# A transformer-layer kernel: unread squares written to SBUF instead of PSUM, the attention transposes one weight tile later, a selection step one chunk earlier

## The chip, the cores and the metric

The kernel runs on one core of one Trainium2 chip. The metric is the device time of one execution in microseconds (us), given as the median over runs. A core has several engines that run their own instruction streams and meet at semaphores: PE (TensorE: matmuls and transposes), DVE (VectorE), ACT (ScalarE), POOL (GpSimd) and SP (here it only issues transfers between device memory and SBUF, the on-chip memory). Matmuls write to PSUM, which has eight banks.

## The reference

One layer of a flow-matching backbone is computed for 384 tokens: 128 context tokens and 256 latent tokens, in three blocks of 128. The width is 2048.

```python
mod = silu(cond) @ ada_w + ada_b           # six modulation vectors per token group
h   = rmsnorm(x) * (1 + scale) + shift     # "ada": scale and shift out of mod
q, k, v, o, gates, u = split(h @ w_in)     # 8 heads x 128; u feeds the pooling
for each head and each of two directions:  # chunkwise mLSTM, chunks of 128
    s   = (q k^T) * exp(dmat - m_t)
    num = g * (q C) + s v                  # "inter" and "intra" part
    den = g * (q n) + sum(s)
    h_d = num / max(|den|, exp(-m_t))
    C   = g_state * C + wk^T v             # new state
h_head = rmsnorm(h_fwd + h_bwd) * w
mix = concat(h_head * sigmoid(o), pooled(u)) @ w_out
x   = x + gate * rmsnorm(mix)
y   = x + gate2 * rmsnorm(relu(rmsnorm_mod(x) @ w1)**2 @ w2)
```

All is in 32-bit floats. To keep that precision on TensorE, each large operand is split into a rounded high part and a remainder, and each product is made of three matmuls: high with high, high with low, low with high.

## The kernel before, in words

**Splitting and weights.** `load_w` (line 114) loads one weight tile of up to 128x1024 numbers into a `raw` buffer (three of them) through SP. ACT copies it to the rounded `hi` tile (L126), DVE subtracts to get `lo` (L127). PE then runs the three products: L394 to L396 in the first stage, L135 to L137 elsewhere. In `gemm_T` (line 158) one weight tile gives 24 matmuls of 128x384 results, and after each weight tile the function calls its *feeds*: generators that each emit the next piece of some other work, up to their next `yield`. So the attention, the modulation vectors and the pooling are woven between the weight tiles of the large products.

**Who sets the order.** The order of each engine's instructions up to line 379 is written by hand. From there a scheduler orders them for each engine, on the basis of the order in which the code emits them and of its own estimates. Buffers that are used in turn (tiles with `bufs=N`, and the eight PSUM banks that `bank` hands out) add waits: whoever takes a buffer again waits for its last user.

**The stages.**

1. Up to about 40 us: loads, transposes of x, the first modulation step.
2. To about 190 us: eight steps over the contraction index, each with five chunks of weights: u_0, u_512, v_0, v_3, v_6 (list `chunks`, line 345). The operand of step s+1 is made by `make_h` (line 347, called at L400 after chunk v_3): it scales and shifts by `mod`, with high parts `hh` from ACT (L358) and low parts `hl` from DVE (L359). `mod` for that step comes from `ada_mat` (line 203), which is resumed `ADA_STEPS[ci]` times after chunk number ci. With (4, 0, 4, 1, 0) that is four weight pieces with their matmuls (L221) after u_0, four after v_0, and one last step after v_3. The step that loads the eighth piece also ends with the copy of the sums to SBUF, `ada_sb` (L226, ACT). The last, ninth step is two small selection matmuls (L229) and `ada_finish` (DVE, L237).
3. To about 265 us: q and k of head pair 0, with the pooling and the gates.
4. To about 408 us: q and k of pairs 1, 2 and 3, with the attention of pairs 0, 1 and 2 as a feed; to about 498 us: the four `o` products, the attention of pair 3 in the first two of them.
5. To about 634 us: the output projection (`wo`), then the MLP to the end.

Through stages 4 and 5 a second feed, `ada_vec` (line 247), makes further modulation vectors on DVE (L268, 1.1 us each).

**One attention pair** (`attention`, line 544) has two heads, `hl` 0 and 1. After each weight tile of the pair's q and k products (four tiles each), it emits one piece: decays (`mb` matmuls L561, exponentials L563); scores and keys; the same for the third block; state updates and `outputs(0)`; `outputs(1)`; `outputs(2)`; an empty piece; the transposes. Then a last piece is empty, and `fa.finish()` (L704) emits whatever is left before the next pair begins.

`outputs(i)` (line 609) takes for each head a bank `num` and, for i > 0, a bank `inter`. PE writes the intra sums to `num` (L616) and the inter sums to `inter` (L623); ACT scales the latter into an SBUF tile `nsb` (L625), and DVE adds `num` to it (L626). After that `num` of PSUM is read no more. DVE and ACT make the denominator (L628 to L630) and the normalised sum `hs` (L631, L632). L633 then squares `hs` on ACT, for the sum of squares in `ssh`; its elementwise result is never read, and goes to the free end of the bank `num`, columns 260 to 387. The sums become a reciprocal root (DVE L187, POOL L188), and DVE scales `hs` by it (L635). The transposes `hT` (L670, three blocks for each of two heads) turn `hs` for the output projection, and ACT copies them out as `hnT` (L672).

Of the kernel before, what the change touches and what calls it, by code (L numbers as in the profile page):

```python
# [9 lines left out]
AF = mybir.ActivationFunctionType  # L10
# [6 lines left out]
NTOK = 384  # L17
NH = 8
M = 1024
# [8 lines left out]
N_W = 4  # L28
N_ADA = 4
N_E = 1  # L30
ADA_STEPS = (4, 0, 4, 1, 0)
X_ORDER = "tatatatabtatatatat"
N_X = 2
RATES = (1.5, 1.3, 1.3)
# [4 lines left out]
def hymba_kernel(  # L39
# [6 lines left out]
    nc = tc.nc  # L46
    w_in, w_out, w1, w2, ada_w = w_in[0], w_out[0], w1[0], w2[0], ada_w[0]
# [10 lines left out]
    def bank(name):  # L58
        return psum.tile([P, 512], F32, tag="ps", name=name)
# [74 lines left out]
    def mm3(ps, lh, ll, rh, rl, start, stop):  # L134
        nc.tensor.matmul(ps, lh, rh, start=start, stop=False)  # L135
        nc.tensor.matmul(ps, lh, rl, start=False, stop=False)  # L136
        mm3.ins = nc.tensor.matmul(ps, ll, rh, start=False, stop=stop).ins  # L137

    def wview(w):
        return w.rearrange("(k p) n -> p k n", p=P)  # L140
# [17 lines left out]
    def gemm_T(w, cols, xs, n, evac, feeds=(), korder=(0, 1, 2, 3), name="g", hold=None):  # L158

        wv = wview(w)  # L160
        acc = {}
        for g, c0 in enumerate(cols):
            for o in range(2):
                acc[g, o] = bank(f"acc_{name}_{c0}_{o}")
        for ki, kc in enumerate(korder):
            for g, c0 in enumerate(cols):
                hi, lo = load_w([(0, wv[:, 4 * kc:4 * kc + 4, c0:c0 + 256])], f"{name}_{c0}_{kc}", after=hold(ki, g) if hold else ())
                for k in range(4):
                    xh, xl = xs(4 * kc + k)
                    for o in range(2):  # L170
                        mm3(acc[g, o][:, 0:n], hi[:, k, o * P:(o + 1) * P], lo[:, k, o * P:(o + 1) * P],
                            xh[:, 0:n], xl[:, 0:n], ki == 0 and k == 0, ki == 3 and k == 3)
                for f in feeds:
                    f()
        for g, c0 in enumerate(cols):
            for o in range(2):
                evac(c0 // P + o, acc[g, o])
# [7 lines left out]
    def rstd_cols(out, ss, n, scale):  # L185

        nc.vector.tensor_scalar(out, ss, scale, EPS, op0=ALU.mult, op1=ALU.add)  # L187
        nc.gpsimd.tensor_tensor(out, out, mhalf[:, 0:n], op=ALU.pow)  # L188
# [193 lines left out]
    for s in range(NS):  # L382
        for ci, (kind, c0, w) in enumerate(chunks):
# [6 lines left out]
            for k in range(nk):  # L390
                xh, xl = h[k0 + k]
                for i in range(3):
# [3 lines left out]
                    nc.tensor.matmul(acc[i][:, 0:n], xl[:, sl], hi[:, k, :], start=False, stop=k == nk - 1)  # L396
            for _ in range(ADA_STEPS[ci]):
                next(ada0, None)
# [14 lines left out]
    hx = lambda k: h[k]  # L413
# [117 lines left out]
    ssh = vp.tile([P, 3, 8], F32, name="ssh")  # L531
# [12 lines left out]
    def attention(hp):  # L544
# [64 lines left out]
        def outputs(i):  # L609
            hs = att.tile([P, 2, P], F32, tag="hs", name=f"hs_{hp}_{i}", bufs=3)  # L610
            for hl in range(2):
                hd = h0 + hl
                ps = bank(f"num_{hp}_{i}_{hl}")
                num = ps[:, 0:260].rearrange("p (d e) -> p d e", e=130)[:, :, 0:129]
                for d in range(2):
                    nc.tensor.matmul(num[:, d], e[:, d, hl, i, :], vsb[i][:, hd, :], start=True, stop=True)  # L616
                if i > 0:
                    pi = bank(f"inter_{hp}_{i}_{hl}")
                    iv = pi[:, 0:260].rearrange("p (d e) -> p d e", e=130)[:, :, 0:129]
                    intra, num = num, att.tile([P, 2, 129], F32, tag="num", name=f"nsb_{hp}_{i}_{hl}", bufs=2)  # L620
                    for d in range(2):
                        cs = C0[d] if tokc[d][1] == i else C1[d]
                        nc.tensor.matmul(iv[:, d], q_sb[hd][:, i * P:(i + 1) * P], cs[:, hl, :], start=True, stop=True)  # L623
                    for d in range(2):
                        nc.scalar.activation(num[:, d], iv[:, d], AF.Copy, scale=gcol[:, i, d, hd:hd + 1])  # L625
                    nc.vector.tensor_tensor(num, num, intra, op=ALU.add)  # L626
                dn = att.tile([P, 2], F32, tag="dn", name=f"dn_{hp}_{i}_{hl}", bufs=4)
                nc.scalar.activation(dn, num[:, :, 128], AF.Abs)  # L628
                nc.vector.tensor_tensor(dn, dn, ecol[:, i, hd, :], op=ALU.max)
                nc.vector.reciprocal(dn, dn)  # L630
                nc.scalar.activation(hs[:, hl, :], num[:, 0, 0:128], AF.Copy, scale=dn[:, 0:1])  # L631
                nc.vector.scalar_tensor_tensor(hs[:, hl, :], num[:, 1, 0:128], dn[:, 1:2], hs[:, hl, :], op0=ALU.mult, op1=ALU.add)  # L632
                nc.scalar.activation(ps[:, 260:388], hs[:, hl, :], AF.Square, accum_out=ssh[:, i, hd:hd + 1])  # L633
            rstd_cols(rsh[:, i, h0:h0 + 2], ssh[:, i, h0:h0 + 2], 2, 1.0 / P)
            nc.vector.tensor_tensor(hs, hs, rsh[:, i, h0:h0 + 2].unsqueeze(2).to_broadcast([P, 2, P]), op=ALU.mult)  # L635
            hss[i] = hs
# [17 lines left out]
        for d, wk in enumerate((wk00, wk01)):  # L654
            o = update(0, d, wk)
            nc.gpsimd.dma_start(new_C[0, 0, d, h0:h0 + 2].rearrange("h k e -> k h e"), o[:, :, 0:128])
            nc.vector.tensor_copy(nout[:, d, h0:h0 + 2], o[:, :, 128])
        C1[0] = update(1, 0, wk10)
        C1[1] = update(2, 1, wk21)
        outputs(0)  # L660
        yield
        for i in (1, 2):
            outputs(i)
            yield
        yield
        for hl in range(2):
            hd = h0 + hl
            ps = bank(f"hT_{hp}_{hl}")
# [6 lines left out]
    def mid_vec():  # L675
        for i, q in ((4, 0), (4, 1), (3, 0), (3, 1), (2, 0)):
            yield from ada_vec(i, 1024 * q, 1024, att)

    ada1 = Feed(ada_mat([(2, 8 + 2 * b, 2) for b in range(4)]), RATE_MAT)
    ada2 = Feed(mid_vec(), RATES[0])  # L680

    def qk(g, feeds):
        gemm_T(w_in, [g * 256], hx, NTOK, evac_q, feeds, name="q")
        gemm_T(w_in, [M + g * 256], hx, NTOK, evac_k, feeds, name="k")
# [13 lines left out]
    pre_scope.close()  # L698
    att_scope = ExitStack()
    att = att_scope.enter_context(tc.tile_pool(name="att", bufs=2))  # L700
    for g in range(1, 4):
        fa = Feed(attention(g - 1), 1.0)
        qk(g, (fa, ada1, ada2))
        fa.finish()  # L704


    ada2.rate = RATES[1]
# [8 lines left out]
    def split_pool():  # L716
        for k in range(8, 16):
            mixs[k] = split_T(mix[k][:, 0:NTOK], f"mx{k}")
            mix[k] = None
            yield  # L720

    fa, fs = Feed(attention(3), 1.0), Feed(split_pool(), 1.0)
    for g in range(4):
        gemm_T(w_in, [3 * M + g * 256], hx, NTOK, evac_o, (fa if g < 2 else fs, ada1, ada2), name="o")
        if g == 1:
            fa.finish()
    fs.finish()

    ps = bank("ps_nout")
# [367 lines left out]
```

## Time and profile before

| what | value |
|---|---|
| runs | 1741.73, 1744.26, 1746.68 us; median 1744.26 |
| profiled execution: own time | 1740.87 us |
| profiled execution: span from the first to the last instruction | 1739.2 us |
| busy: PE / DVE / ACT / POOL | 97% / 62% / 36% / 9% of the span |
| mean granted TensorE clock | 0.996 of full speed |

A row of a timeline gives the start on the span's clock, the time that the group took, the engine, the line of the kernel, and the operation with what it writes and reads (`out<-in`); in brackets stands how long the engine was idle before it and what released it. "PEld" is the loading of weights into the array, which overlaps with the matmuls. A row of the waits names who waited, for whom, the total in us, how often, and the longest. A row of the windows gives the busy time and the count of each engine in a stretch of the span, then the mean granted clock (`PEclk`), the mean share of the DMA engines that was busy, and the rate in GB/s.

### The profile page before, as it was taken

What the parts mean: (1) busy time and instruction counts of PE and PEld (TensorE: products, weight loads), DVE (VectorE), ACT (ScalarE), POOL (GpSimd) and SP (SyncE); (2) the same over time, 40 slices, a digit from 0 to 9 for tenths busy, and PEclk for the clock granted to TensorE, in tenths of its full rate; (3) what the DMA queues carried; (4) which work ended last, traced back from release to release, by engine and by line L of the source; (5) the groups of instructions that cost most, each with busy time, mean ns of one, the idle gap of its engine ahead of it and who ended that gap; (6) DMA issues with size and microseconds to landing.
All of it is one profiled execution on the core that took longest, in us unless ns stands there. A gap on an engine that the chain in (4) does not pass through costs nothing.

```text
span 1739.2 us, 24241 instructions
## 1 busy us (share of the span) xinstructions
PE 1695.3 (97%) x9461; PEld 1528.6 (88%) x9461; DVE 1084.5 (62%) x1620; ACT 630.4 (36%) x1050; POOL 150.5 (9%) x186
## 2 busy tenths in 40 slices
PE   6999999999999999999999999999999999999997
PEld 3888898988899989989988988988988988998986
DVE  3677759787889959997347543457444444443446
ACT  4422344545433336443322322322322332332332
POOL 0000002211002223530000000000000000000100
PEclk9999999999999999999999999999999999999999
DMA  9888857776668893755446534444444435434543
GB/s 300 292 291 292 286 164 238 229 227 220 222 216 265 267 317 114 217 162 181 122 125 187 160 122 133 122 148 151 125 122 131 124 122 174 130 121 143 173 133 108
DMA packets 235266, 320.71 MB, mean 184 GB/s; under 512 B 14368, under 2 KB 177808, under 8 KB 234768
## 3 DMA queue, kind: packets, MB, share of 16 engines
q1 hardware_dynamic: 227760, 303.61, 55.6%
q0 software_dynamic: 5728, 13.69, 2.9%
q10 hardware_dynamic: 1664, 1.87, 0.3%
q8 instruction: 74, 1.21, 0.3%
q14 instruction: 40, 0.33, 0.1%
HBM read 308.61 MB, written 10.51 MB: 183 GB/s over the span
## 4 chain that ended last, share of the span: by engine, by line
PE 77%; DVE 9%; DMA 6%; issue 6%; POOL 1%; ACT 1%; SPq 0%; DVEq 0%; POOLq 0%; ACTq 0%
PE y L901 10%; PE y L902 10%; PE y L903 10%; PE acc_w L136 9%; PE acc_w L137 9%; PE acc_w L135 9%; DVE ada_acc L268 4%; PE ada L221 2%; DMA raw_u<-in_w_in_dram 1%; DMA raw_v<-in_w_in_dram 1%; PE acc_q L135 1%; PE acc_o L135 1%; PE acc_q L136 1%; PE acc_q L137 1%; PE acc_o L137 1%
## 5 line engine op out<-in xcount | busy, mean ns | idle before, releaser
L127 DVE TENSOR_TENSOR lo_w<-raw_w,hi_w 128x1024 fp32r<-128x1024 f32 x256 | 313.3, 1224 | 404.2 <-ACT hi_w L126 403.7
L126 ACT ACTIVATE hi_w<-raw_w 128x1024 fp32r<-128x1024 f32 x256 | 271.1, 1059 | 563.9 <-PE y L903 273.1
L136 PE MATMUL acc_w<-h2l,hi_w 128*128 128x384 f32 (+1 forms) x1024 | 346.2, 338 | 0.5 <-DVE h2l L857 0.5
L137 PE MATMUL acc_w<-h2h,lo_w 128*128 128x384 f32 (+1 forms) x1024 | 345.5, 337 | 0.0
L135 PE MATMUL acc_w<-h2h,hi_w 128*128 128x384 f32 (+1 forms) x1024 | 343.7, 337 | 0.7 <-ACT h2h L853 0.6
L268 DVE SCALAR_TENSOR_TENSOR ada_acc<-ada_raw,sg,ada_acc 128x1024 f32<-128x1024 f32 (+1 forms) x240 | 257.2, 1108 | 2.8 <-DMA ada_raw<-in_ada_w_dram 2.7
L135 PEld LDWEIGHTS acc_w<-h2h,hi_w 128*128 128x128 f32 x1024 | 192.2, 188 | 2.3 <-ACT h2h L853 1.5
L136 PEld LDWEIGHTS acc_w<-h2l,hi_w 128*128 128x128 f32 x1024 | 192.5, 188 | 1.7 <-DVE h2l L857 0.8
L137 PEld LDWEIGHTS acc_w<-h2h,lo_w 128*128 128x128 f32 x1024 | 192.4, 188 | 0.1
L806 DVE TENSOR_TENSOR z<-z 128x384 f32<-128x384 f32 x54 | 30.0, 556 | 53.6 <-ACT z L805 53.4
L925 DVE TENSOR_TENSOR y<-y,y 128x512 f32<-128x512 f32 x81 | 55.6, 691 | 11.3 <-PE y L903 10.9
L126 ACT ACTIVATE hi_wo<-raw_wo 128x1024 fp32r<-128x1024 f32 x32 | 34.0, 1063 | 77.3 <-DMA raw_wo<-in_w_out_dram 37.5
L819 POOL DMA_DIRECT2D gf_dram<-gfT x1 | 0.5, 521 | 669.3 <-DVE gfT L818 669.3
L805 ACT ACTIVATE z<-acc_w 128x384 f32<-128x384 f32 x54 | 26.3, 488 | 75.7 <-PE acc_w L137 75.7
L394 PE MATMUL v<-hi_v,hh 128*128 128x384 f32 (+1 forms) x144 | 47.7, 332 | 0.0
L221 PE MATMUL ada<-ada_raw,cT 128*32 128x256 f32 x672 | 46.0, 395 | 1.1 <-DMA ada_raw<-in_ada_w_dram 1.1
L127 DVE TENSOR_TENSOR lo_wo<-raw_wo,hi_wo 128x1024 fp32r<-128x1024 f32 x32 | 41.0, 1292 | 9.2 <-ACT hi_wo L126 8.8
L396 PE MATMUL v<-hi_v,hl 128*128 128x384 f32 (+1 forms) x144 | 46.5, 323 | 0.0
L395 PE MATMUL v<-lo_v,hh 128*128 128x384 f32 (+1 forms) x144 | 46.5, 323 | 0.0
L135 PE MATMUL acc_o<-hh,hi_o 128*128 128x384 f32 x128 | 44.8, 350 | 0.0
L135 PE MATMUL acc_q<-hh,hi_q 128*128 128x384 f32 x128 | 44.7, 349 | 0.0
L135 PE MATMUL acc_k<-hh,hi_k 128*128 128x384 f32 x128 | 44.4, 347 | 0.0
(957 smaller groups left out, 3634.5 us busy)
## 6 DMA issues: line engine op xcount, KB each, us to landing
raw_w<-in_w_dram SPq DMA_DIRECT2D x256, 512.0 KB, 3.8
ada_raw<-in_ada_w_dram SPq DMA_DIRECT2D x188, 512.0 KB, 4.8
raw_wo<-in_w_out_dram SPq DMA_DIRECT2D x32, 512.0 KB, 5.0
raw_u<-in_w_in_dram SPq DMA_DIRECT2D x16, 512.0 KB, 7.9
raw_q<-in_w_in_dram SPq DMA_DIRECT2D x16, 512.0 KB, 4.5
raw_k<-in_w_in_dram SPq DMA_DIRECT2D x16, 512.0 KB, 5.0
raw_o<-in_w_in_dram SPq DMA_DIRECT2D x16, 512.0 KB, 4.7
raw_v<-in_w_in_dram SPq DMA_DIRECT2D x16, 384.0 KB, 8.1
```

What stands on the lines that cost most here:

```text
L126: nc.scalar.activation(hi[:, 0:n], raw[:, 0:n], AF.Copy)
L127: low = lambda: nc.vector.tensor_tensor(lo[:, 0:n], raw[:, 0:n], hi[:, 0:n].bitcast(F32), op=ALU.subtract)
L135: nc.tensor.matmul(ps, lh, rh, start=start, stop=False)
L136: nc.tensor.matmul(ps, lh, rl, start=False, stop=False)
L137: mm3.ins = nc.tensor.matmul(ps, ll, rh, start=False, stop=stop).ins
L221: nc.tensor.matmul(ps[32 * g:32 * g + 32, 0:w], cT[:, j, 6 - 2 * b:38 - 2 * b], raw[:, a, :], start=b == 0 and j < 4, stop=b == n - 1 and ...
L268: nc.vector.scalar_tensor_tensor(acc[:, g, :], raw[:, a, :], cj, acc[:, g, :], op0=ALU.mult, op1=ALU.add)
L394: nc.tensor.matmul(acc[i][:, 0:n], xh[:, sl], hi[:, k, :], start=k == 0, stop=False)
L901: nc.tensor.matmul(acc, xh[:, s], hi, start=k == 8 * ch, stop=False)
L902: nc.tensor.matmul(acc, xh[:, s], lo, start=False, stop=False)
L903: nc.tensor.matmul(acc, xl[:, s], hi, start=False, stop=k == 8 * ch + 7)
L925: nc.vector.tensor_tensor(dst, acc[i], dst, op=ALU.add)
```

## The change

Three things are changed.

- **The scratch of the squares.** For i > 0, L633 writes the unread squares to the SBUF tile `nsb` (the half that L632 has just read), where it wrote them to the PSUM bank `num`. The bank is then free after DVE's addition L626. For i = 0, `num` is the PSUM bank itself, and nothing changes.
- **The transposes.** `attention` has one more `yield` ahead of the transposes, so a pair now takes nine pieces. The pairs' feeds are kept in the list `fa`, the last two are passed on to each pair of products, and `fa.finish()` is gone. The ninth piece comes after the first weight tile of the *next* product, beside the next pair's first piece.
- **The selection.** `ADA_STEPS` is (4, 0, 5, 0, 0): the ninth step of `ada_mat` comes after chunk v_0, right behind the eighth; `make_h` stays after chunk v_3.

The lines behind the inserted `yield` have a number higher by one: `hT` is L671 in the changed kernel, `hnT` L673.

```diff
-ADA_STEPS = (4, 0, 4, 1, 0)
+ADA_STEPS = (4, 0, 5, 0, 0)
...
-                nc.scalar.activation(ps[:, 260:388], hs[:, hl, :], AF.Square, accum_out=ssh[:, i, hd:hd + 1])
+                nc.scalar.activation(num[:, 1, 0:128] if i > 0 else ps[:, 260:388], hs[:, hl, :], AF.Square, accum_out=ssh[:, i, hd:hd + 1])
...
             outputs(i)
             yield
         yield
+        yield
         for hl in range(2):
...
+    fa = []
     for g in range(1, 4):
-        fa = Feed(attention(g - 1), 1.0)
-        qk(g, (fa, ada1, ada2))
-        fa.finish()
+        fa.append(Feed(attention(g - 1), 1.0))
+        qk(g, (*fa[-2:], ada1, ada2))
...
-    fa, fs = Feed(attention(3), 1.0), Feed(split_pool(), 1.0)
+    fa.append(Feed(attention(3), 1.0))
+    fs = Feed(split_pool(), 1.0)
     for g in range(4):
-        gemm_T(w_in, [3 * M + g * 256], hx, NTOK, evac_o, (fa if g < 2 else fs, ada1, ada2), name="o")
-        if g == 1:
-            fa.finish()
+        gemm_T(w_in, [3 * M + g * 256], hx, NTOK, evac_o, (*fa[2:], *((fs,) if g >= 2 else ()), ada1, ada2), name="o")
```

**PE at the end of attention pair 0.** Before: the last matmul of k (`acc_k`), then the transposes `hT` of the blocks 0 and 1, then the first matmuls of the next pair's q (`acc_q`), then the transposes of block 2.

```order
L137 MATMUL acc_k_1_2888<-hh_1864,lo_k_3_3080 128x384
L670 MATMUL hT_0_3107<-cst,hs_0_2845 128x128
L670 MATMUL hT_0_3107<-cst,hs_1_2919 128x128
L670 MATMUL hT_1_3113<-cst,hs_0_2845 128x128
L670 MATMUL hT_1_3113<-cst,hs_1_2919 128x128
L135 MATMUL acc_q_0_3131<-hh_262,hi_q_0_3135 128x384
L136 MATMUL acc_q_0_3131<-hl_263,hi_q_0_3135 128x384
L137 MATMUL acc_q_0_3131<-hh_262,lo_q_0_3136 128x384
L135 MATMUL acc_q_1_3132<-hh_262,hi_q_0_3135 128x384
L136 MATMUL acc_q_1_3132<-hl_263,hi_q_0_3135 128x384
L670 MATMUL hT_0_3107<-cst,hs_2_2991 128x128
L670 MATMUL hT_1_3113<-cst,hs_2_2991 128x128
```

In the changed kernel the 24 matmuls of q's first weight tile come first; these are the last of them and what follows (`mb` are the next pair's decays).

```order
L137 MATMUL acc_q_1_3120<-hh_496,lo_q_0_3124 128x384
L671 MATMUL hT_0_3151<-cst,hs_0_2845 128x128
L671 MATMUL hT_0_3151<-cst,hs_1_2919 128x128
L671 MATMUL hT_0_3151<-cst,hs_2_2991 128x128
L671 MATMUL hT_1_3157<-cst,hs_0_2845 128x128
L671 MATMUL hT_1_3157<-cst,hs_1_2919 128x128
L671 MATMUL hT_1_3157<-cst,hs_2_2991 128x128
L561 MATMUL mb_0_0_3171<-mrow,pick 128x384
L561 MATMUL mb_0_1_3176<-mrow,pick 128x384
L561 MATMUL mb_1_0_3181<-mrow,pick 128x384
L135 MATMUL acc_q_0_3119<-hh_719,hi_q_1_3203 128x384
L136 MATMUL acc_q_0_3119<-hl_720,hi_q_1_3203 128x384
```

The first transposes moved back by 24 matmuls and the last two by 19. The other three pairs move alike; for pairs 2 and 3 the product that follows is one of the `o` products.

**PE in the u and v stage, step 2.** Before: the end of the 18 matmuls of chunk v_3 (the tile `v_2_2` of them), then the selection L229, then chunk v_6.

```order
L394 MATMUL v_2_2_922<-hi_v_2_916,hh_724 128x384
L395 MATMUL v_2_2_922<-lo_v_2_917,hh_724 128x384
L396 MATMUL v_2_2_922<-hi_v_2_916,hl_725 128x384
L229 MATMUL ada_6_800<-cst,ada_sb_6_909 128x4 x2
L394 MATMUL v_2_0_974<-hi_v_2_970,hh_719 128x288
```

In the changed kernel: the end of the modulation matmuls L221, the first three matmuls of chunk v_3, and then the selection.

```order
L221 MATMUL ada_6_800<-ada_raw_6_12_903,cT 32x256 x4
L394 MATMUL v_2_0_925<-hi_v_2_921,hh_719 128x384
L395 MATMUL v_2_0_925<-lo_v_2_922,hh_719 128x384
L396 MATMUL v_2_0_925<-hi_v_2_921,hl_720 128x384
L229 MATMUL ada_6_800<-cst,ada_sb_6_909 128x4 x2
L394 MATMUL v_2_1_926<-hi_v_2_921,hh_719 128x384
```

The selection moved ahead by 15 of the 18 matmuls. It reads `ada_sb`.

**ACT at the same place.** Before: the copy of the last chunk's weights, `ada_sb`, the copy of the next step's first u weights (`hi_u_3`), the four parts of `hh`, the second u weights.

```order
L126 ACTIVATE hi_v_2_970<-raw_v_2_967 128x576
L226 ACTIVATE ada_sb_6_909<-ada_6_800 128x256
L126 ACTIVATE hi_u_3_1003<-raw_u_3_1001 128x1024
L358 ACTIVATE hh_947<-hm_946,mod 128x128
```

In the changed kernel:

```order
L126 ACTIVATE hi_v_2_970<-raw_v_2_967 128x576
L126 ACTIVATE hi_u_3_1003<-raw_u_3_1001 128x1024
L226 ACTIVATE ada_sb_6_909<-ada_6_800 128x256
L126 ACTIVATE hi_u_3_1058<-raw_u_3_1056 128x1024
L358 ACTIVATE hh_947<-hm_946,mod 128x128
```

`ada_sb` now stands behind the copy of the next step's first u weights, in each of steps 2 to 6. On SP the loads moved with it: before, one u tile and two v tiles follow the first half of the modulation pieces, one v tile and one u tile the second half; in the changed kernel the three v tiles follow the first half and the two u tiles the second.

## The prediction

> **What bounds the kernel now.** I read the page's head first, then PE's waits, then a table of windows, then the timeline around each wait.
>
> ```profile
> span 1739.2 us, 24241 instructions
> PE 1695.3 (97%) x9461; PEld 1528.6 (88%) x9461; DVE 1084.5 (62%) x1620; ACT 630.4 (36%) x1050; POOL 150.5 (9%) x186
> ```
>
> PE works for all but 43.9 us of the span. No matmul of weights is taken away here, so the change can gain only what PE idles, or what it runs below full clock. The waits of PE between 40 and 600 us say how much lies near the change:
>
> ```profile
> PE hT L670 <- DVE hs L635: 7.1, 4, 2.3
> PE inter L623 <- ACT num L633: 5.3, 4, 2.3
> PE u L394 <- ACT hh L358: 1.9, 1, 1.9
> PE acc_wo L137 <- DVE lo_wo L127: 0.9, 2, 0.8
> ```
>
> The columns are total, count and longest. The transposes wait once for each of the four attention pairs (7.1 us in all); `inter`, whose bank L633 still writes, four times (5.3); the first u matmul once, for `hh` (1.9). Together that is 14.3 us. The windows show which stages are tight for DVE, and where the clock falls:
>
> ```profile
> 40.00:160.00 120.00, 119.91 (x871) 97.19 (x870) 82.26 (x169) 39.93 (x66) 1.26 (x3) 1.00 0.90 294
> 280.00:320.00 40.00, 36.41 (x239) 33.92 (x238) 36.31 (x65) 20.33 (x61) 11.45 (x9) 1.00 0.77 241
> 320.00:360.00 40.00, 37.72 (x246) 35.29 (x245) 29.96 (x63) 18.16 (x50) 7.01 (x7) 0.97 0.68 211
> 360.00:400.00 40.00, 38.75 (x252) 37.45 (x252) 34.88 (x55) 18.45 (x55) 7.94 (x8) 0.99 0.76 235
> 400.00:440.00 40.00, 38.10 (x241) 35.58 (x239) 29.24 (x52) 18.41 (x45) 5.23 (x5) 0.96 0.65 207
> 440.00:480.00 40.00, 36.57 (x230) 34.16 (x229) 36.75 (x58) 18.70 (x47) 3.06 (x3) 1.00 0.71 230
> 520.00:560.00 40.00, 39.10 (x224) 38.21 (x226) 40.00 (x32) 14.65 (x22) 10.29 (x5) 1.00 0.84 267
> ```
>
> After the window's length come PE, PEld, DVE, ACT and POOL, then clock, DMA share and GB/s. In pairs 1 and 2 (320 to 440 us) DVE has 5 to 11 us to spare in 40. In pair 0 (280 to 320) and pair 3 (440 to 480) it has about 3.5, and at 520 to 560, in the output projection, none.
>
> **Part 1: the transposes, one weight tile later.** Pair 1 in the timeline:
>
> ```profile
> 354.78 0.60 PE L670 MATMUL hT<-cst,hs 128*128 128x128 f32 x4
> 355.49 1.66 POOL L188 TENSOR_TENSOR rsh<-rsh,mhalf 128x2 f32<-128x2 f32 x1 [8.13 <-DVE rsh L187]
> 357.18 0.42 DVE L635 TENSOR_TENSOR hs<-hs,rsh 128x256 f32<-128x256 f32 x1 [0.58 <-POOL rsh L188]
> 357.66 0.69 PE L670 MATMUL hT<-cst,hs 128*128 128x128 f32 x2 [2.28 <-DVE hs L635]
> 358.47 0.52 PE L136 MATMUL acc_q<-hl,hi_q 128*128 128x384 f32 x1
> 358.79 0.52 PE L137 MATMUL acc_q<-hh,lo_q 128*128 128x384 f32 x1
> 361.18 0.34 PE L136 MATMUL acc_q<-hl,hi_q 128*128 128x384 f32 x1
> 361.36 0.34 PE L137 MATMUL acc_q<-hh,lo_q 128*128 128x384 f32 x1
> ```
>
> PE reaches the transposes at 354.78, and the last scaled `hs` is there at 357.60 (357.18 + 0.42). At full clock the matmuls start 0.18 us apart (361.18, 361.36). The 24 that now stand ahead take about 24 x 0.175 = 4.2 us, against 2.3 us of stall, so in pair 1 the wait is gone. Right after the stall matmuls start 0.32 us apart (358.47, 358.79): the clock is about half. Its price follows from the windows: 320 to 360 lacks 0.03 of 40 us and 360 to 400 lacks 0.01, so 1.6 us; 400 to 440, with the stall of pair 2, lacks 0.04, again 1.6 us. Without the stalls I expect neither dip. The weight load of the transpose loses some 0.2 us more. Pair 1: 2.3 + 0.2 + 1.6, about +4.1.
>
> A rule of the Trainium skill bears on the dips ("TensorE: Matmul & The Clock Gate", section "Why this matters for your kernels"): the clock halves after about 3 us without matmuls. By that rule stalls of 2.3 us would not cost the clock, and the sum would be 3.2 us smaller if the dips had another cause and stayed; the row of 358.47 stands directly behind the stall, and I go by it.
>
> Pairs 0, 2 and 3, by the rows of PE that waited and what they waited for:
>
> ```profile
> 292.29 0.75 DVE L626 TENSOR_TENSOR nsb<-nsb,num 128x258 f32<-128x258 f32 x2
> 293.76 0.39 PE L616 MATMUL num<-v,e 128*128 128x129 f32 x2
> 295.97 0.28 ACT L633 ACTIVATE num<-hs 128x128 f32<-128x128 f32 x1 [0.17 <-DVE hs L632]
> 296.43 0.71 PE L623 MATMUL inter<-C,q 128*128 128x129 f32 x4 [2.28 <-ACT num L633]
> 306.13 0.60 PE L670 MATMUL hT<-cst,hs 128*128 128x128 f32 x4
> 307.96 0.42 DVE L635 TENSOR_TENSOR hs<-hs,rsh 128x256 f32<-128x256 f32 x1 [0.59 <-POOL rsh L188]
> 308.44 0.44 PE L670 MATMUL hT<-cst,hs 128*128 128x128 f32 x2 [0.83 <-DVE hs L635]
> 389.41 0.71 PE L623 MATMUL inter<-C,q 128*128 128x129 f32 x4 [1.25 <-ACT num L633]
> 407.36 0.66 PE L670 MATMUL hT<-cst,hs 128*128 128x128 f32 x4 [1.90 <-DVE hs L635]
> 442.29 0.71 PE L623 MATMUL inter<-C,q 128*128 128x129 f32 x4 [1.30 <-ACT num L633]
> 461.06 0.44 PE L670 MATMUL hT<-cst,hs 128*128 128x128 f32 x2 [2.13 <-DVE hs L635]
> ```
>
> **Part 2: the scratch of the squares.** In pair 0 PE waits from 294.15 to 296.43 for L633 (295.97), while DVE's last read of that bank, L626, ended at 293.04 (292.29 + 0.75). With the scratch in SBUF this wait ends before PE arrives, so 2.3 us go; in pairs 2 and 3 likewise 1.25 and 1.30. The fourth wait, the rest of the 5.3 us (0.5), is at a block with i = 0, which is unchanged. L633 took 0.28 us into PSUM; into SBUF I bound it by L631's 0.40, the next rows' ACT tile of that size: 0.1 us x 16 on an engine that is half idle (20.33 of 40 us), so nothing on the path, or 1.9 us if all were.
>
> ```profile
> L633 ACT ACTIVATE num<-hs 128x128 f32<-128x128 f32 x24 | 6.7, 279 | 14.3 <-DVE hs L632 14.3
> L631 ACT ACTIVATE hs<-nsb,dn 128x128 f32<-128x128 f32 x16 | 6.3, 396 | 3.1 <-DVE dn L630 3.0
> ```
>
> By pair, then. **Pair 0:** 2.3 + 0.2 (weight load) for `inter`. PE then comes 2.5 us earlier and meets the transposes at 306.13 - 2.5 + 4.2 = 307.8, but DVE, busy without a pause here, still has `hs` at 308.4 or a little before. I leave 0.3 us of stall of the 0.83 + 0.2: 2.5 + 0.7 = +3.2. **Pair 2:** 1.25 + 0.2, 1.90 + 0.2 and the clock 1.6: +5.1. **Pair 3:** 1.30 + 0.2, 2.13 + 0.2: 3.8 at its own place, but DVE follows without slack into the output projection, where PE already waits for `lo_wo` (0.9 us). PE that arrives earlier will wait there for the same DVE instruction; I keep 0.5 (bounds 0 and 3.8).
>
> A new wait of part 1: the bank of the fourth `mb` of the next pair is the one that ACT reads for `hnT`, just behind the transposes. The scheduler set that `mb` two matmuls later (0.35 us); the two `hnT` copies take 1.05 us together at 358.17. I take 0.15 us x 3 = -0.5 (bounds 0 and -1.6).
>
> **Part 3: the selection, 15 matmuls earlier.** The gain is the `hh` wait of 1.9 us in the last step, plus about 0.3 of lighter waits for `lo_u`: `mod` is there earlier and `make_h` runs ahead. The price lies on ACT and SP: `ada_sb` now stands behind the copy `hi_u` of the next step, which waits for its load. A step of before:
>
> ```profile
> 112.09 1.93 PE L221 MATMUL ada<-ada_raw,cT 128*32 128x256 f32 x32
> 113.46 0.68 ACT L126 ACTIVATE hi_v<-raw_v 128x576 fp32r<-128x576 f32 x1 [8.04 <-DMA raw_v<-in_w_in_dram]
> 114.09 0.39 ACT L226 ACTIVATE ada_sb<-ada 128x256 f32<-128x256 f32 x1
> 114.68 1.06 ACT L126 ACTIVATE hi_u<-raw_u 128x1024 fp32r<-128x1024 f32 x1 [0.20 <-DMA raw_u<-in_w_in_dram]
> ```
>
> PE ends the modulation matmuls at 114.02 and three matmuls later, at 114.6, wants the selection. If `raw_u` lands as before (114.68), `hi_u` ends at 115.74, `ada_sb` at 116.13, and PE stalls some 1.6 us. But the load of v_6 (295 KB) no longer stands ahead of it, which at the window's 294 GB/s is 1.0 us, and the swap in the first half (a 295 KB tile for one of 524 KB) brings the modulation pieces up to 0.8 us forward. The stall is then 0 to 0.6 us, I take 0.3, and five steps are so ordered: -1.5. Part 3 in all: 2.2 - 1.5 = +0.7 (bounds -5.8, with 1.6 us in each of the five, and +2.2).
>
> **The sum.** 3.2 + 4.1 + 5.1 + 0.5 - 0.5 + 0.7 = 13.1 us. The profiled execution's own time, 1740.87 us, becomes 1727.8. The median of the runs is 1744.26, 3.4 us above that execution, and on it the forecast is 1731.2.
>
> **Rivals.** *All of it counts.* DVE catches up in the o stage, pair 3 keeps its 3.8, and the selection never waits: 3.3 + 1.5 + 0.5 more, a gain of 18.4, 1725.9. For it: DVE idles in 400 to 440 (29.24 of 40). Against: 40.00 of 40 at 520 to 560.
>
> *DVE is the bound behind the transposes.* The transposes wait again one weight tile later since DVE, with PE earlier, is late by what was won before. Kept would be the `inter` waits of pairs 0 and 2 (2.5 + 1.5) and one tile's cover in pair 1 (2.5), less part of the rest: 6.5 us, 1737.8. For it: 36.31 busy of 40 in pair 0. Against: 29.96 and 29.24 in pairs 1 and 2.
>
> *Slower: the selection stalls PE in the u and v stage.* There PE has no idle now (119.91 of 120), and the loads run at 0.90 of the DMA engines. If raw_u lands as late as before, five stalls of 1.6 us come; if each brings a clock dip of 1.6 us as the stall of 357.66 did, and delays the release of the `ada` buffers and with it the next loads by as much again, the price is 5 x (1.6 + 1.6 + 1.6) = 24 us, against 14.6 us of gains elsewhere (13.1 + 1.5): slower by 9, 1753. It decides from a loss of 3 us a step on. Against: raw_u gets a shorter queue ahead of it.
>
> *The change doesn't do what it says.* If the bank of `num` were held by another reader, the `inter` waits would stay: 13.1 - 2.5 - 1.5 = 9.1 us, 1735.2. The order of instructions leaves L626 as the last user, so little speaks for it.
>
> **How the numbers follow.** A measurement tells some 0.3%, 5.2 us, from no change. I give 0.55 to the forecast with its bounds (gain 9 to 16), 0.16 to the full gain, 0.17 to DVE as the bound (a third of it within 5.2 us), 0.05 to the bank that stays held, 0.07 to stalling selections (0.04 slower, 0.03 about even). Faster: 0.55 + 0.16 + 0.11 + 0.05 = 0.87; same: 0.06 + 0.03 = 0.09; slower 0.04. The range goes from the full gain with some margin, 1724, to DVE as the bound, 1738.
>
> **What would show it.** Right: `inter` waits for L633 only at i = 0 (0.5 us); `hT` waits for `hs` under 1 us in all; PEclk 1.00 in all windows from 320 to 440; the waits for `lo_wo` up by 2 to 3 us; selections that wait 0.3 us behind `ada_sb`, and no wait of u for `hh`. Wrong: waits of `hT` above 3 us in all (DVE), PE under 116 of 120 us in the window 40 to 160 (selection), or a clock under 1.00 where no stall stands.

## The result and the profile after

The changed kernel takes 1733.32 us (median of 6 runs, 1730.40 to 1734.16) against 1742.99 us before (median of 6, 1738.11 to 1746.68). The ratio is 0.9944, with a 95% interval from 0.9925 to 0.9963: 9.7 us faster. The forecast was 1731.2, a gain of 13.1.

The head of the profile after, whose execution took 1733.51 us:

```profile
span 1731.8 us, 24241 instructions
PE 1693.1 (98%) x9461; PEld 1527.8 (88%) x9461; DVE 1082.6 (63%) x1620; ACT 629.1 (36%) x1050; POOL 150.6 (9%) x186
```

PE's idle time fell from 43.9 to 38.7 us. PE's waits between 25 and 640 us, in total, count and longest (left out are 1.4 us for `lo_u` and 1.0 of `ps_col`, both as before, and 0.4 for a load of a modulation piece):

```profile
PE ada L229 <- ACT ada_sb L226: 4.4, 4, 1.4
PE inter L623 <- ACT num L633: 2.0, 2, 1.2
PE acc_wo L137 <- DVE lo_wo L127: 1.0, 2, 0.8
PE inter L623 <- DVE C L606: 0.9, 1, 0.9
PE acc_k L135 <- ACT C L603: 0.8, 1, 0.8
PE mb L561 <- ACT hnT L673: 0.5, 1, 0.5
```

The 7.1 us of the transposes and the 1.9 of `hh` are gone, and `inter` waits 2.0 us for L633 where it waited 5.3. New are 4.4 us of the selection and 2.2 us behind the states C and `hnT`. The windows of the changed kernel, columns as before:

```profile
40.00:160.00 120.00, 117.92 (x841) 95.22 (x844) 81.05 (x167) 38.04 (x63) 1.25 (x3) 0.99 0.88 288
160.00:200.00 40.00, 37.57 (x248) 31.07 (x241) 28.37 (x62) 12.51 (x20) 0.00 (x0) 0.96 0.80 266
280.00:320.00 40.00, 39.41 (x256) 37.63 (x255) 37.02 (x63) 20.29 (x61) 7.93 (x7) 1.00 0.77 239
320.00:360.00 40.00, 40.00 (x271) 37.27 (x270) 32.12 (x68) 19.80 (x54) 11.69 (x9) 1.00 0.74 236
360.00:400.00 40.00, 37.08 (x244) 35.13 (x244) 36.35 (x56) 18.96 (x57) 7.56 (x8) 1.00 0.78 242
400.00:440.00 40.00, 39.28 (x259) 36.48 (x258) 32.98 (x59) 20.77 (x54) 5.62 (x6) 1.00 0.67 216
440.00:480.00 40.00, 40.00 (x249) 38.19 (x248) 38.50 (x58) 18.72 (x45) 3.06 (x3) 1.00 0.80 254
```

The clock is at 1.00 from 280 to 480 us, and short in the u and v stage instead (0.99 of 120 us, 0.96 of 40). PE has full windows at 320 and 440; it has lost ground at 40 to 160 (117.92 against 119.91) and in pair 2 (37.08 against 38.75).

By stage, from the starts of first matmuls in the timelines: from the first u matmul to the k product of pair 1 (the u and v stage and the products up to the window of pair 0; called the first stretch below) the execution before took 250.3 us and the one after 256.6; from there to the output projection 216.4 and 205.0; from there to the end 1241.2 and 1239.5. So the attention gave 11.4 us, and in these two executions the first stretch took 6.2 back. That last number is too large for the change: with the order of before, the first stretch took from 250.3 to 256.3 us in nine executions (that of before and eight of the experiments), 253.0 in the mean, and the one of before is the shortest. The spread goes with the clock: the executions that met no dip to half clock there took 250.3 to 251.2 us (three), those with one dip 253.0 to 253.7 (four), those with two 255.6 and 256.3. The one after met two. This is why the two profiled spans lie 7.4 apart and the medians 9.7.

### The profile page after: what moved, and what is told of

It is laid out like the page before. It is cut to its first block, busy times and chain, and to the rows that moved or that the text cites. A ratio compares the mean times of both kernels' runs of the same rounds, so it can differ in the third digit from the quotient of the medians.

```text
span 1731.8 us, 24241 instructions
## 1 busy us (share of the span) xinstructions
PE 1693.1 (98%) x9461; PEld 1527.8 (88%) x9461; DVE 1082.6 (63%) x1620; ACT 629.1 (36%) x1050; POOL 150.6 (9%) x186
## 4 chain that ended last, share of the span: by engine, by line
PE 76%; DVE 9%; DMA 8%; issue 4%; ACT 1%; POOL 1%; SPq 0%; DVEq 0%; ACTq 0%; POOLq 0%
PE y L901 10%; PE y L903 10%; PE y L902 10%; PE acc_w L135 9%; PE acc_w L136 9%; PE acc_w L137 9%; DVE ada_acc L268 4%; DMA raw_u<-in_w_in_dram 3%; PE acc_o L135 1%; PE acc_o L137 1%; PE acc_o L136 1%; PE acc_q L135 1%; PE acc_q L137 1%; DMA raw_v<-in_w_in_dram 1%; PE acc_q L136 1%
## 5 line engine op out<-in xcount | busy, mean ns | idle before, releaser
L268 DVE SCALAR_TENSOR_TENSOR ada_acc<-ada_raw,sg,ada_acc 128x1024 f32<-128x1024 f32 (+1 forms) x240 | 258.2, 1111 | 0.8 <-DMA ada_raw<-in_ada_w_dram 0.7
L925 DVE TENSOR_TENSOR y<-y,y 128x512 f32<-128x512 f32 x81 | 55.5, 691 | 11.1 <-PE y L903 10.8
L805 ACT ACTIVATE z<-acc_w 128x384 f32<-128x384 f32 x54 | 26.3, 488 | 75.5 <-PE acc_w L137 75.5
L221 PE MATMUL ada<-ada_raw,cT 128*32 128x256 f32 x672 | 45.7, 392 | 1.6 <-DMA ada_raw<-in_ada_w_dram 1.5
```

Source lines behind the costliest of these rows:

```text
L268: nc.vector.scalar_tensor_tensor(acc[:, g, :], raw[:, a, :], cj, acc[:, g, :], op0=ALU.mult, op1=ALU.add)
L925: nc.vector.tensor_tensor(dst, acc[i], dst, op=ALU.add)
```

## The experiments

Theory 1, formed from the profile after: the attention's gain comes from the transposes; the squares gain little, since what they free is waited for again one step later, at the transposes, by the chain through DVE; the selection loses, since `ada_sb` stands behind a copy that waits for a load. The rival: the terms add, as the prediction summed them. All ratios are to the kernel before, run beside it on the same chip; its medians beside the three groups of experiments were 1742.85, 1742.95 and 1744.67 us.

**One part at a time.** The selection alone:

```diff
-ADA_STEPS = (4, 0, 4, 1, 0)
+ADA_STEPS = (4, 0, 5, 0, 0)
```

> Before, with only the selection moved (ADA_STEPS (4, 0, 5, 0, 0)). Theory 1 (the selection stalls): PE waits 4 to 5 us for ada_sb between 60 and 190 us, one or two stretches of half clock (1.6 us each) follow, the hh wait of 1.9 us is gone: 6 us slower than before, 1.003 to 1.004. Rival (the stalls seen in the changed kernel are given back later, as PE waits less in the attention): within 2 us of before, 0.999 to 1.001.

Measured: 1742.74 us, ratio 1.0002 (0.9988 to 1.0016). The stalls are there, but not the 6 us: by the time the rival was closer. PE's waits of the profiled execution, in which `ada_sb` takes 5.0 us and `hh` none:

```profile
PE hT L670 <- DVE hs L635: 5.9, 3, 2.1
PE ada L229 <- ACT ada_sb L226: 5.0, 5, 2.7
PE inter L623 <- ACT num L633: 4.5, 4, 2.3
```

The profiled execution took 256.0 us for the first stretch, 3.0 more than the mean of the order of before; the waits of the attention were a little shorter. For the u and v stage alone, from the first u matmul to the first q matmul, it took 178.8 us, and the changed kernel 179.4; the nine executions with the order of before took 173.2 to 177.6, 175.3 in the mean.

The squares alone:

```diff
-                nc.scalar.activation(ps[:, 260:388], hs[:, hl, :], AF.Square, ...)
+                nc.scalar.activation(num[:, 1, 0:128] if i > 0 else ps[:, 260:388], hs[:, hl, :], AF.Square, ...)
```

> Before, with only the unread squares moved to SBUF. Theory 1 (DVE sets when the transposes can run): the inter waits go (5.3 to about 1 us), but in pairs 0, 2 and 3 the transposes wait longer by nearly as much (7.1 to 10 or 11 us): 1 us faster, 0.999 to 1.000, and the clock dips stay. Rival (the terms add): 5 us faster, 0.997, transposes still wait 7 us.

Measured: 1743.35 us, ratio 1.0001 (0.9989 to 1.0013). The wait of `inter` in pair 0 went and the transposes waited longer, as theory 1 has it:

```profile
PE hT L670 <- DVE hs L635: 9.6, 4, 3.2
PE inter L623 <- ACT num L633: 1.3, 2, 0.8
```

All of the growth is in pair 0: in pairs 2 and 3 the transposes wait 1.9 and 2.1 us, as before. There the waits of `inter` could not go. The rows of before tell which square each wait of `inter` hangs on:

```profile
295.59 0.35 DVE L632 SCALAR_TENSOR_TENSOR hs<-nsb,dn,hs 128x128 f32<-128x128 f32 x1
388.57 0.35 DVE L632 SCALAR_TENSOR_TENSOR hs<-num,dn,hs 128x128 f32<-128x128 f32 x1
441.45 0.60 DVE L632 SCALAR_TENSOR_TENSOR hs<-num,dn,hs 128x128 f32<-128x128 f32 x2
```

The first stands just ahead of the wait of 2.28 us in pair 0 and reads `nsb`: a block with i > 0, whose square moves. The other two stand ahead of the waits at 389.41 (pair 2) and 442.29 (pair 3) and read `num` in PSUM: the first block, i = 0, whose square the change leaves where it is. So of the 5.3 us only 2.3 hung on a square that moves. The two that stay are 0.8 and 0.5 us here, 1.25 and 0.72 in the changed kernel.

What became of the 2.3 us shows in pair 0. First the row of the first scaled `hs` in the kernel before (that of the last, at 307.96, stands in the prediction), then the first and the last with the squares alone, and the transposes there.

```profile
291.95 0.43 DVE L635 TENSOR_TENSOR hs<-hs,rsh 128x256 f32<-128x256 f32 x1 [0.62 <-POOL rsh L188]
```

```profile
293.36 0.43 DVE L635 TENSOR_TENSOR hs<-hs,rsh 128x256 f32<-128x256 f32 x1 [0.62 <-POOL rsh L188]
...
309.38 0.43 DVE L635 TENSOR_TENSOR hs<-hs,rsh 128x256 f32<-128x256 f32 x1 [0.59 <-POOL rsh L188]
...
309.86 0.69 PE L670 MATMUL hT<-cst,hs 128*128 128x128 f32 x2 [3.20 <-DVE hs L635]
```

From the first to the last it takes 16.0 us in both. Over these 16.0 us DVE has nearly no pause in the kernel before; the window's columns are as above, so DVE is busy for 14.81 us, 8.92 of them in seven of the L268:

```profile
291.95:307.96 16.01, 13.37 (x86) 12.17 (x85) 14.81 (x32) 7.77 (x23) 4.02 (x3) 1.00 0.69 214
```

DVE's chain does not get shorter when `inter` runs 2.3 us earlier, so PE, which needs the end of that chain, gains nothing there. The stall of 0.83 us became 3.20, and met a dip of the clock (PEclk 0.96 from 280 to 320 us, 1.00 before). The attention of this one execution, from the window of pair 0 to the output projection, took 213.9 us against 216.4, all of the difference behind the start of the `o` products; the whole runs, from 1.9 us faster to 2.3 slower, do not confirm a gain.

The transposes alone (the squares and the selection as before):

```diff
         yield
+        yield
         for hl in range(2):
...
-        qk(g, (fa, ada1, ada2))
-        fa.finish()
+        qk(g, (*fa[-2:], ada1, ada2))
...
```

> Before, with only the transposes one weight tile later. Theory 1: the transposes no longer wait (7.1 to under 1 us), no dips of the clock between 320 and 440 us, but the inter waits for L633 stay at 5 us or grow to 7: 7 to 9 us faster, 0.995 to 0.996. Rival (PE runs into DVE elsewhere, so that cover alone brings nothing): 0 to 3 us faster, new waits for lo and C.

Measured: 1735.05 us, ratio 0.9947 (0.9932 to 0.9962), by the ratio 9.2 us faster: theory 1. No wait of the transposes is left among PE's waits, and the inter waits stay:

```profile
PE inter L623 <- ACT num L633: 4.2, 3, 2.3
PE u L394 <- ACT hh L358: 2.0, 2, 1.8
PE acc_k L135 <- ACT C L603: 1.0, 1, 1.0
```

Squares and transposes, without the selection:

```diff
-ADA_STEPS = (4, 0, 5, 0, 0)
+ADA_STEPS = (4, 0, 4, 1, 0)
```

> The changed kernel with the selection back behind chunk v_3 (ADA_STEPS (4, 0, 4, 1, 0)): squares and transposes alone. Theory 1 (the attention's gain of 11 us holds, the selection costs 6): 1731 against a before of 1743, 0.993, and 4 to 6 us faster than the changed kernel. Rival (what the selection loses, PE gets back in the attention by waiting less for DVE): as the changed kernel, 0.9944, with more waits for DVE and C in pair 2.

Measured: 1731.77 us, ratio 0.9936 (0.9921 to 0.9950). The time is what theory 1 said, but the changed kernel is only 1.4 us behind by the two ratios, not 4 to 6, and the intervals overlap. With the 0.3 us of the selection alone, its cost in whole runs is not clear of noise. This execution met an `hh` wait of 3.7 us in the u and v stage, and from the window of pair 0 to the output projection it took 205.9 us, against 206.2 with the transposes alone: the squares add 0.3 us there.

**What makes the selection wait.** One step of the changed kernel:

```profile
112.17 1.50 PE L221 MATMUL ada<-ada_raw,cT 128*32 128x256 f32 x24
114.43 1.06 ACT L126 ACTIVATE hi_u<-raw_u 128x1024 fp32r<-128x1024 f32 x1 [9.10 <-DMA raw_u<-in_w_in_dram]
115.39 0.36 ACT L226 ACTIVATE ada_sb<-ada 128x256 f32<-128x256 f32 x1
115.81 0.61 PE L229 MATMUL ada<-cst,ada_sb 128*128 128x4 f32 x4 [1.41 <-ACT ada_sb L226]
```

ACT stood idle for 9.10 us until `raw_u` landed, while `ada_sb`, whose input was ready when L221 ended at 113.67, queued behind. The prediction had `raw_u` land 1.0 to 1.8 us earlier against the modulation matmuls than before; here it is 0.8 us *after* their end, before it was 0.7. So the queue ahead was shorter by a load, but nothing was won. The test puts `ada_sb` ahead of the copy:

```diff
-        nc.scalar.activation(sb[:, 0:w], ps[:, 0:w], AF.Copy)
+        sb_ins.append(nc.scalar.activation(sb[:, 0:w], ps[:, 0:w], AF.Copy).ins)
...
-load_chunk(s, ci, h_ins if s == 0 else ())
+load_chunk(s, ci, h_ins if s == 0 else sb_ins[-1:] if ci == 0 else ())
```

> The changed kernel with one thing set in ACT's order: ada_sb stands ahead of the next step's first hi_u in each step, as in before; the selection stays behind the first three matmuls of chunk v_3. Theory 1 (the place behind hi_u makes the selection wait): the waits of L229's matmuls for ada_sb (4.4 us, up to 1.4) fall under 0.6 us, PE is busy at least 119.5 of 120 us in the window 40 to 160, no hh wait: 3 to 5 us faster than the changed kernel, 1728 to 1730, 0.992. Rival (the loads or PE's own early arrival set it): the selection still waits 3 us or more, within 1 us of the changed kernel.

More than ACT's order changed, since the scheduler answered: in most steps 15 of the u matmuls moved from ahead of the first half of the modulation matmuls to behind it, and on SP three loads of v moved behind four loads of modulation pieces. So the test does not set the place of `ada_sb` alone.

Measured: 1730.73 us, ratio 0.9932 (0.9912 to 0.9953), 2.6 us under the changed kernel's median; the intervals of the ratios overlap. In the profile the wait of the selection goes, as theory 1 has it, though PE's window of 117.65 missed the expected 119.5:

```profile
PE ada L223 <- DMA ada_raw<-in_ada_w_dram: 1.9, 5, 0.8
PE ada L231 <- ACT ada_sb L228: 0.7, 2, 0.6
```

```profile
40.00:160.00 120.00, 117.65 (x853) 93.66 (x852) 80.61 (x167) 37.45 (x63) 1.26 (x3) 1.00 0.90 287
```

The selection's wait fell from 4.4 to 0.7 us, `hh` is not waited for, the clock has no dip between 40 and 640 us. But the modulation matmuls, half of which PE now reaches 15 matmuls earlier, wait for their own loads (1.9 us). The first stretch took 252.3 us, against 256.6: 4.2 better than the changed kernel, and no better than the mean of before (253.0). The two other kernels with `ada_sb` first, further down, took 251.0 and 255.8 there. For the u and v stage alone the three took 175.2, 173.8 and 177.1 us, 175.3 in the mean as with the order of before, where the two with `ada_sb` behind `hi_u` took 179.4 and 178.8. I take the loads, at 0.90 of the DMA engines, for the next bound there; no run tests that.

**DVE: its load, or what stands ahead in its queue?** Half of the columns of L268 left out, beside before, the squares alone, and squares with transposes:

```diff
-    nc.vector.scalar_tensor_tensor(acc[:, g, :], raw[:, a, :], cj, acc[:, g, :], ...)
+    m = n // 2 if n == 1024 else n
+    nc.vector.scalar_tensor_tensor(acc[:, g, 0:m], raw[:, a, 0:m], cj, acc[:, g, 0:m], ...)
```

> Before, with half the columns left out of the multiply-adds of the modulation vectors that are made beside attention and output projection (L268 on 128x512, for all but the first term); the output's modulation is wrong in these columns. It is the reference for the next two. Theory 1 (DVE's queue sets when hs is ready): the transposes wait 3 to 4 us and not 7.1, 3 to 5 us faster than before, 0.997 to 0.998. Rival (the chain over ACT and POOL sets it, whatever DVE has to do): they wait 6 to 7 us, within 1.5 us of before.

Measured: 1737.26 us, ratio 0.9967 (0.9951 to 0.9982), within theory 1's range. The shorter L268 also led the scheduler to another order on PE, DVE, ACT and SP than that of before; the lightened kernel with the squares moved has the order of the lightened before.

> The same lightened DVE, with the squares moved to SBUF and nothing else. Theory 1 (the squares gave nothing alone because DVE was the next to be waited for): now the inter waits go and the transposes' wait grows by less than half of it: 2 to 4 us faster than the lightened before. Rival (the chain behind the transposes takes it back without DVE too): within 1 us of the lightened before.

Measured: 1738.74 us, ratio 0.9983 (0.9968 to 0.9997): theory 1 missed, 1.5 us slower than the lightened before with overlapping intervals. The squares gave nothing that the runs can tell, with light DVE work as well. PE's waits in the lightened before, and then with the squares moved:

```profile
PE inter L624 <- ACT num L634: 4.9, 2, 3.6
PE hT L671 <- DVE hs L636: 3.9, 2, 3.4
```

```profile
PE hT L671 <- DVE hs L636: 7.3, 3, 3.2
PE inter L624 <- ACT num L634: 1.2, 1, 1.2
```

DVE in pair 0 of the latter:

```profile
296.44 0.75 DVE L269 SCALAR_TENSOR_TENSOR ada_acc<-ada_raw,sg,ada_acc 128x512 f32<-128x512 f32 x1 [1.45 <-DMA ada_raw<-in_ada_w_dram]
...
300.48 0.75 DVE L269 SCALAR_TENSOR_TENSOR ada_acc<-ada_raw,sg,ada_acc 128x512 f32<-128x512 f32 x1 [0.55 <-DMA ada_raw<-in_ada_w_dram]
```

In these rows (the lightened kernels number their lines one higher) DVE, with less to do, waits inside its queue for the loads of the modulation pieces, and the chain of `hs` waits behind. From the first to the last scaled `hs` of pair 0 it took 18.2 us in the lightened before and 17.0 here, with eight of these multiply-adds between them where before has seven. Less work per instruction did not empty the queue ahead of the chain.

> The same lightened DVE, with squares and transposes moved, the selection as in before. Theory 1: all PE waits for DVE and ACT between 280 and 500 us are under 2 us together (the kernel with full DVE work has 4.5), 8 to 10 us faster than the lightened before, PE busy over 39.3 of 40 us in each window from 280 to 480. Rival: the new waits for C, for L633 at the first block and for L603 stay at 4 us, since weights' loads and not DVE set them.

Measured: 1728.67 us, ratio 0.9919 (0.9898 to 0.9940), 8.6 us under the lightened before, as theory 1 has it, with 1.7 us of waits left for C and L633 in the attention. PE was busy 39.06 to 40.00 of 40 us in the windows from 280 to 480, in two of them a little under the 39.3 expected.

So the next two kernels take that work out of the way of pairs 0 and 1 altogether:

```diff
-RATES = (1.5, 1.3, 1.3)
+RATES = (0.0, 1.3, 1.3)
```

> Before, with the feed of the modulation vectors (ada_vec) set to rate 0 beside q and k of pairs 1 to 3, so that DVE has none of L268 beside attention pairs 0 and 1; they are made later, in the output projection, which costs there. Theory 1 (what holds hs is the work that stands ahead of its chain in DVE's in-order queue): from the first to the last L635 of pair 0 it takes 14 us or less (16.0 in before, and 16.0 with the squares moved), and the transposes of pairs 0 and 1 wait under 1.5 us in all (3.1 in before). Rival (ACT, POOL and the weights' loads set the chain): 16 us again, and 3 us or more of waits. The whole is 5 us or more slower in both.

Measured: 1803.36 us, ratio 1.0336 (1.0317 to 1.0356); 57.8 us of waits for L268 appear later, in the output projection, as that work must be done there. The windows of pairs 0 and 1, and the first and last scaled `hs` of pair 0:

```profile
280.00:320.00 40.00, 40.00 (x268) 38.20 (x266) 18.24 (x49) 22.36 (x64) 6.83 (x9) 1.00 0.48 145
320.00:360.00 40.00, 40.00 (x264) 38.60 (x262) 21.81 (x53) 22.72 (x62) 6.75 (x9) 1.00 0.51 156
```

```profile
287.62 0.43 DVE L635 TENSOR_TENSOR hs<-hs,rsh 128x256 f32<-128x256 f32 x1 [1.83 <-POOL rsh L188]
...
298.42 0.42 DVE L635 TENSOR_TENSOR hs<-hs,rsh 128x256 f32<-128x256 f32 x1 [0.80 <-POOL rsh L188]
```

PE idles not at all in these windows, and the chain takes 10.8 us, not 16.0: theory 1. Neither L633 nor the transposes hold PE up in these pairs: both waits came with the L268 that stand in DVE's queue between the steps of the chain. Their loads are gone with them (0.48 of the DMA engines against 0.77), but in before DVE idled only 1.2 of the 16.0 us, each time for POOL, so it was not the loads that the chain waited for. In pairs 2 and 3, where L268 runs again, the transposes wait 2.2 us and `inter` 1.8. The scheduler changed the order of other instructions here too, so the step from 16.0 to 10.8 is not that of the L268 alone.

> The same, with the squares moved to SBUF and no instruction in another place. Theory 1: in pairs 0 and 1 any wait of inter for L633 goes, and since DVE has room the transposes' wait does not grow: pairs 0 and 1 are shorter by what inter waited before, 0 to 2 us. Rival: the transposes wait longer by the same amount and the two pairs take as long as without the squares moved.

Measured: 1804.13 us, ratio 1.0340 (1.0323 to 1.0356). There was nothing left to gain in these pairs, so this run does not part the theory from the rival: from the k product of pair 1 to that of pair 3 it took 90.2 us with and without the squares moved.

**The squares on top of the rest.** With `ada_sb` first, the squares put back into PSUM, and then the first block's squares moved out as well:

```diff
-num[:, 1, 0:128] if i > 0 else ps[:, 260:388]
+ps[:, 260:388]
```

> The changed kernel with ada_sb ahead of hi_u, and the squares of all blocks written to PSUM as in before; no instruction changes its place on any engine, only the wait for L633 returns. Theory 1 (the wait of inter for L633 is covered: the chain over DVE behind it ends at the same time): within 1.5 us of the same kernel with the squares in SBUF (1730.7), 0.993, although inter waits 4 us and not 2.9. Rival (with the transposes out of the way the wait costs its full length): 3 to 4 us slower, 0.995.

Measured: 1733.63 us, ratio 0.9939 (0.9924 to 0.9953); the same kernel with the squares in SBUF had 0.9932. By the medians it is 2.9 us slower, by the ratios 1.2: between theory 1 and the rival. The inter waits are 3.8 us, and from the window of pair 0 to the output projection it took 205.8 us against 204.9.

```diff
+                sqt = num[:, 1, 0:128] if i > 0 else att.tile([P, 2, 129], F32, tag="num", bufs=2)[:, 1, 0:128]
...
-nc.scalar.activation(num[:, 1, 0:128] if i > 0 else ps[:, 260:388], ...)
+nc.scalar.activation(sqt, ...)
```

> The changed kernel with ada_sb ahead of hi_u, and the squares of the first block (i = 0) also written to an SBUF tile. Theory 1 (what is left of the wait, up to 1.2 us each, is for DVE's L632 just before L633): inter waits for L632 and not L633, under 0.5 us shorter each, within 1.5 us of 1730.7, 0.993. Rival (the wait is L633's own): inter waits under 1 us in all, 2 us faster, 1728.7.

Measured: 1731.22 us, ratio 0.9920 (0.9906 to 0.9935), run beside the one above, whose interval it overlaps by a little. The scratch is one of the two `nsb` buffers. The waits moved to L632 (line 635 of this kernel), as theory 1 has it, and to the bank that `hnT` reads; 1.5 us more are left behind the states C:

```profile
PE mb L563 <- ACT hnT L676: 1.1, 1, 1.1
PE inter L625 <- DVE hs L635: 1.0, 2, 0.8
```

Its stage from the window of pair 0 took 204.7 us. So the squares on top of the transposes are worth some 1 us by the stages of single executions (0.3 to 1.1), and 1.2 to 3.3 us by the ratios of whole runs, whose intervals overlap each time. The best kernels here, with `ada_sb` first, reach 0.993 and 0.992.

## Why the prediction was right, and where its steps failed

**Transposes, one tile later: right, and nearly the whole gain.** The wait of 7.1 us went, as did both clock dips of 320 to 440 us; the 24 matmuls cover the stall. The transposes alone gave 9.2 us by their ratio.

**Squares: the step that failed, twice.** "In pairs 2 and 3 likewise 1.25 and 1.30" is a misreading: these waits hang on the square of the first block, which the change does not move, as the rows of 388.57 and 441.45 show. The prediction looked for 0.5 us of waits for L633 that are left, all at i = 0; there are 2.0, all at i = 0. And in pair 0, "with the scratch in SBUF this wait ends before PE arrives, so 2.3 us go": the wait goes, the time does not. Alone the squares gave nothing that the runs can tell (1.0001), on top of the transposes 1 us or a little more, because DVE's queue ended the pair at the same time. In the sum stood 2.5 us for pair 0, 1.45 for pair 2 and, of pair 3's 3.8, only 0.5. The rival "DVE is the bound" had the right mechanism, and asked for it in the wrong place: the transposes, one tile later, stayed clear of it.

**Pair 2: sized 5.1, gave less.** From the start of the k product that runs beside its second half (382.26 and 381.90) to that of the first `o` product (408.52 and 406.47) it took 26.3 us before and 24.6 after. With the dip of 1.6 us that lay behind the old stall this is 3.3 us; 1.45 of the 5.1 were the square that does not move. Beside that old wait (1.25 us at 390.13, at 389.41 before) stand two that the prediction did not name, both for the states C: 0.8 us of `acc_k` and 0.9 of `inter`. Pair 2 in the changed kernel:

```profile
380.52 1.06 ACT L126 ACTIVATE hi_k<-raw_k 128x1024 fp32r<-128x1024 f32 x1 [2.09 <-PE num L616]
381.48 0.64 ACT L603 ACTIVATE C<-cu 128x258 f32<-128x258 f32 x2
387.51 0.61 DVE L606 SCALAR_TENSOR_TENSOR C<-C,glast,cu 128x129 f32<-128x129 f32 x2 [2.32 <-DMA out_dram<-C]
387.91 0.49 PE L623 MATMUL inter<-C,q 128*128 128x129 f32 x2 [0.88 <-DVE C L606]
390.13 0.71 PE L623 MATMUL inter<-C,q 128*128 128x129 f32 x4 [1.25 <-ACT num L633]
```

`hi_k` runs at the time it ran at before (380.25), though PE started the state updates 1.4 us earlier (378.27 and 379.66); L603 stands behind it on ACT, the store of C behind L603, L606 behind the store, `inter` behind L606. So PE waits here for part of what it gained in pair 1. Why that copy ran no earlier is not shown by an experiment: the row's releaser is PE, but the weight load of that tile, issued at 375.62 after and 375.05 before, landed at 380.41 and 380.15, so I take the load to be the cause.

**Pair 3: sized 0.5, kept 2.1.** From the `o` products to the output projection it took 89.5 us before and 85.8 after, of which 1.6 is the dip of pair 2. The wait for `lo_wo` stayed at 1.0 us; it was to grow by 2 to 3. My reading, which no run tests, is that DVE had been held by the same stalls as PE, as its own instructions wait for `inter` and `hT`, and came earlier with it.

**The `mb` wait** was taken at 0.5 us and is 0.5, at one place.

**Selection: sign open, price wrong.** Forecast +0.7 us. By single executions the u and v stage took 3.8 us longer than the mean of before (two executions, each above all nine with the order of before); by whole runs 0.3 and 1.4 us, not clear of nothing. The step that failed is the load that was to land "up to 0.8 us forward" besides the 1.0: the wait was 4.4 us where 1.5 was taken, and in this execution two dips of the clock came with it, one directly behind the row of 115.81:

```profile
116.66 0.53 PE L395 MATMUL v<-lo_v,hh 128*128 128x384 f32 x1
116.98 0.53 PE L396 MATMUL v<-hi_v,hl 128*128 128x384 f32 x1
```

The rival "slower" had named this place; its price per step, 4.8 us, was too high, and the attention's gain covered it.

So the sum, 13.1, came out 3.4 us too high: the transposes carried it. The attention was sized 12.4 in all and gave 11.4 in the two executions, but not part by part: pair 2 gave less and pair 3 more, for reasons that the prediction did not have. That its total came so near is luck.

## What to carry to other kernels

A wait that is taken off the critical engine is worth only what the next wait of the same engine does not take back; to size it, follow the chain that ends at that next wait (here 16.0 us with and without the change) and not the stall. Covering the *last* wait of the chain with independent work was worth 9 us, while removing one inside it was worth nothing that the runs could tell. Before a wait is counted as gone, look in the rows at which write it hangs on: two of the three that were counted here hung on one that the change left alone. Before an instruction is put behind another in an in-order queue, look at what that other one waits for: `ada_sb` had its input at 113.67 and ran at 115.39, behind a copy that had nothing to do with it, and PE waited 1.4 us.

## What the runs showed of the hardware

Stalls well under 3 us were followed by a stretch of half clock: PE idled 1.41 us at 115.81 us in the changed kernel, and the matmuls behind started 0.32 us apart from 116.66 to 119.8. Not all were: the stall of 2.28 us at 296.43 in before had no such stretch behind it (PEclk 1.00 from 280 to 320), that of 2.28 at 357.66 had one. One and the same stall can go either way: PE waits 1.0 us at `ps_col` in each of the fourteen executions, between 223 and 230 us, and from 200 to 240 us PEclk is 0.96 in four of them and 1.00 in ten. The rule of the Trainium skill that the prediction weighed ("TensorE: Matmul & The Clock Gate", section "Why this matters for your kernels"), some 3 us without matmuls, does not hold here as a safe limit. In two of the three kernels with `ada_sb` first no such stretch was found between 40 and 640 us; the third, with the first block's squares moved as well, had two (PEclk 0.99 from 40 to 160 us and 0.96 from 200 to 240). What decides between the two cases was not tested, so a dip that a single execution gains or loses is no measure of a change.
